# W_down of both sequences in one pass of seven block products, with its combinations made in the steps

## The chip, the core and the metric

The kernel runs on one core of a Trainium2 chip. The metric is the time of one execution on the device in microseconds; the median of several runs stands for a kernel. TensorE does the matrix products (in the profile PE, its weight loads PEld), VectorE is DVE, ScalarE is ACT, GpSimd is POOL, and SyncE (SP) issues nearly all transfers, one after the other from one queue.

## What is computed

One layer of a bidirectional encoder on two sequences with the same weights, `x_sample` (512 tokens) and `x_prompt` (1024 tokens), both preceded by 16 meta tokens. All is in 32-bit floats. What the change touches is the end of the layer and the last norm:

```python
D_MODEL = 1024; D_FF = 4 * D_MODEL
...
    x = x + mixed @ w_out
    a = jax.nn.relu(rmsnorm(x, g_mlp) @ w_up)
    return x + (a * a) @ w_down
...
    return rmsnorm(h, g_final)[:, N_META:]
```

## The kernel before

**The two sequences** run one after the other, the sample first. Each goes through projections, attention, the Fourier branch, the merge, `project_out` (W_out, the residual and the norm for the MLP) and the MLP. While the sample's MLP runs, `reading` takes in the prompt's tokens (load, norm, transposition), one tile at a time.

**Precision.** Every product of two 32-bit tiles is made from three matmuls: each operand is split into a high part (rounded by ScalarE, L151) and the low rest (a subtraction by GpSimd or DVE, L152), and `mm3` (L128) adds high x high, high x low and low x high into one PSUM bank. A matmul has a stationary operand of 128 x 128 and a moving one of 128 x 512. A weight block of 128 x 1024 numbers is 512 KB; `wtile` gives two buffers each for a raw block, its high and its low part (`w_raw`, `w_hi`, `w_lo`).

**The sample's MLP** (class `Mlp`) goes over the 4096 hidden channels in 32 blocks of 128. `up(f)` makes block f for all 512 tokens: 8 x 3 matmuls, relu on ScalarE (L1082), the square on DVE (L1083), and the split (L1084, L1085). After every two blocks `down` multiplies them by their two blocks of W_down: 4 tiles of tokens x 2 halves of the output, 6 matmuls each, and DVE adds each result to an accumulator in SBUF (L1131). The last `down` takes four blocks; beside it the four blocks of w_in for the prompt's V (`before_last`) are loaded and split, and the four tiles of tokens get their last norm and are stored.

**Combinations.** While W_down's blocks lie in SBUF for the sample, `combine` makes on GpSimd (L1100) the four block sums that the prompt's product needs, and stores them in DRAM (`wt`, 2 MB for each of eight groups u of 512 hidden channels).

**The prompt's MLP** (class `Halves`) makes products of 2 x 2 blocks with seven block products (Winograd's form): the tokens are cut into two halves of 512, the channels into two halves. `up` makes the hidden channels in 16 pairs, and stores for each group u the four quarters of the squared hidden and four sums of them in DRAM (`hidden_prompt`, L1461 and L1477). Its turn tiles (`take`, names x0 to x7, y0, y1, gain) hold the weights of W_up in turn.

**The prompt's W_down** (`start_down`, `fetch_down`, `down`) then goes through 7 x 8 steps: for each of the seven products n, over the eight groups u. A step loads one quarter or sum of the hidden (512 KB) and one block or combination of W_down (512 KB) (L1496), splits both, and does 4 tiles x 2 x 3 = 24 matmuls. The steps' split parts have four buffers, and `load(i + 3)` is called in step i. When the last u of a product is done, `evict` puts the four banks together into the accumulators. The last three steps of the last product are done tile by tile, and each tile is normed and stored (`finish`) at once.

**Order.** A planner orders the instructions of each engine ahead of time by their place in the program and by its own estimate of when each can start, so that an instruction can be put ahead of earlier ones that are not ready. `behind(marks)` and `pinned()` hold instructions behind what stands before them in the program on the same engine.

Of the kernel before, what the change touches and what calls it, by code (L numbers as in the profile page):

```python
# [17 lines left out]
F32 = mybir.dt.float32  # L18
# [50 lines left out]
class Layer:  # L69
    def __init__(self, tc, ctx, ins, outs):  # L70
# [17 lines left out]
        self.wt = []  # L88
# [239 lines left out]
    def run(self, order):  # L328
# [3 lines left out]
        for i, (name, T) in enumerate(order):  # L332
# [112 lines left out]
            mlp = self.Mlp(self, hp_, mp, name, T, h2T, acc)  # L445
# [18 lines left out]
            mlp.run(reading, before_last, gate, lambda: tile_("r1").bitcast(F32))  # L464
# [546 lines left out]
    def project_out(self, hp, p, x, T, m, wo, acc, mlp, marks):  # L1011
# [36 lines left out]
        mlp.load(2, self.pair(p, [128, 2, 512], "w", 2))  # L1048
# [5 lines left out]
    class Mlp:  # L1054
        G = 2
        NF = FF // 128

        def __init__(self, layer, hp, p, name, T, h2T, acc):
            self.layer, self.nc, self.hp, self.p, self.name, self.T, self.h2T, self.acc = layer, layer.nc, hp, p, name, T, h2T, acc
            self.w, self.hid = {}, {}  # L1060
            self.ups = [self.up(f) for f in range(self.NF)]

        def load(self, f, to=None):
            if f not in self.w:
                to = to and [x.rearrange("p a (k c) -> p (a k) c", c=128) for x in to]
                self.w[f] = self.layer.weights(self.layer.rows("w_up", f * 128), to)

        def up(self, f):
# [4 lines left out]
            hi, lo = (t.rearrange("p a b -> p (a b)") if len(t.shape) == 3 else t  # L1073
                      for t in self.layer.pair(self.hp, [128, T] if T == 512 else [128, 2, 512], "hid", 2 * self.G))
            self.hid[f] = hi, lo
            step = 256 if f < 3 and T == 512 else 512
            for c in range(T // step):
# [3 lines left out]
                r = self.p.tile([128, 512], F32, name="relu", bufs=2)[:, :step]  # L1081
                nc.scalar.activation(out=r, in_=ps, func=AF.Relu)  # L1082
                nc.vector.tensor_tensor(out=r, in0=r, in1=r, op=ALU.mult)  # L1083
                nc.scalar.copy(out=hi[:, cs], in_=r)  # L1084
                nc.vector.tensor_tensor(out=lo[:, cs], in0=r, in1=hi[:, cs].bitcast(F32), op=ALU.subtract)  # L1085
                yield

        def combine(self, g, even, odd):


            nc, wt = self.nc, self.layer.wt
            if g % 2 == 0:
                wt.append(self.layer.dram.tile([128, 2, 4, 512], F32, name=f"wt{g // 2}"))
            (b11, b12), (b21, b22) = ([x[:, i] for i in range(2)] for x in (even, odd))
            t = [self.hp.tile([128, D], F32, name="hn", bufs=2) for _ in range(2)]
            t1, t2, t3, t4 = (x[:, i * 512:(i + 1) * 512] for x in t for i in range(2))
            to = [wt[-1][:, g % 2, 2 * i:2 * i + 2].rearrange("p a b -> p (a b)") for i in range(2)]
            for i, ops in enumerate((((t1, b12, b11), (t2, b22, t1)), ((t3, b22, b12), (t4, b21, t2)))):
                for x in ops:
                    nc.gpsimd.tensor_tensor(out=x[0], in0=x[1], in1=x[2], op=ALU.subtract)  # L1100
                nc.sync.dma_start(to[i], t[i])
                yield

        def down(self, fs, last, gate):

            layer, nc, T, acc, hid = self.layer, self.nc, self.T, self.acc, self.hid
            w, raws = {}, []
            marks = layer.mark()
            for i, f in enumerate(fs):
                to = (layer.pair(self.p, [128, 2, 512], "w", 2 if T == 512 else 4) if i < 2 else  # L1110
                      tuple(gate()[:, :, :512] for _ in range(2)))
                raw = self.raws[i]().rearrange("p (a b) -> p a b", a=2)
                nc.sync.dma_start(raw, layer.ins["w_down"][f * 128:(f + 1) * 128, :].rearrange("p (a b) -> p a b", a=2))
                w[f] = [t.rearrange("p a b -> p (a b)") if T == 512 else t for t in layer.split_sb(raw, *to)]
                raws.append(raw)
            combining = chain(*(self.combine(fs[i] // 2, raws[i], raws[i + 1]) for i in range(0, len(fs), 2)))
            if last:
                for _ in combining:
                    pass
                with layer.behind(marks + layer.mark()):  # L1120
                    last()
                gain = layer.gain(self.p.tile([128, D], F32, name="gain", bufs=1), "g_final")
            for t in range(T // 128):
                ts = slice(t * 128, (t + 1) * 128)
                for half in range(2):
                    cs = slice(half * 512, (half + 1) * 512)
                    ps = layer.psum()
                    layer.mm3(ps, [(hid[f][0][:, ts], hid[f][1][:, ts], *(v[:, cs] if T == 512 else v[:, half] for v in w[f]))
                                   for f in fs])
                    with layer.tc.high_priority(offset=60) if last and t == T // 128 - 1 else nullcontext():  # L1130
                        nc.vector.tensor_tensor(out=acc[t][:, cs], in0=acc[t][:, cs], in1=ps, op=ALU.add)  # L1131
                with layer.pinned():
                    next(combining, None)
                if last:
                    o = self.hp.tile([128, D], F32, name="hn", bufs=2)
                    with layer.tc.high_priority(offset=60) if t == T // 128 - 1 else nullcontext():
                        layer.norm(acc[t], gain, o, junk=self.p.tile([128, D], BF16, name="junk", bufs=1))
                    nc.sync.dma_start(layer.outs[self.name][t * 128:(t + 1) * 128, :], o)

        def run(self, reading, before_last, gate, raw):  # L1140
            other = lambda: self.layer.wtile("raw", [128, D]).bitcast(F32)
            self.raws = [raw, lambda: self.p.tile([128, D], F32, name="gain", bufs=1), other, other]
            G, NF = self.G, self.NF
            for g in range(NF // G - 1):
                for f in range(g * G + (G if g else 0), (g + 2) * G):
                    for _ in self.ups[f]:
                        pass
                next(reading, None)
                if g < NF // G - 2:
                    self.down(range(g * G, (g + 1) * G), None, gate)  # L1150
            for _ in reading:
                pass
            self.down(range(NF - 2 * G, NF), before_last, gate)


class Halves:
# [18 lines left out]
    def run(self, right, hp, mp, m, wo):  # L1175
# [6 lines left out]
        raws = [list(layer.pair(mp, [128, 2, self.TH], "w", 2)) for _ in range(2)]  # L1182
        self.start_down(raws)
# [297 lines left out]
    DOWN = ((0, "b11", 0), (5, "t2", 1), (2, "b21", 0), (6, "t3", 1), (4, "t1", 0), (3, "t4", 1), (7, "b22", 0))  # L1481

    def block(self, b, u):

        if b[0] == "t":
            return self.layer.wt[u][:, :, int(b[1]) - 1]
# [4 lines left out]
    def fetch_down(self, i, raws):  # L1491

        n, u = self.steps[i]
        a, b, _ = self.DOWN[n]
        for raw, src in zip(raws, (self.hid[u][:, :, a], self.block(b, u))):
            self.nc.sync.dma_start(raw.bitcast(F32), src)  # L1496
        self.raws[i] = raws
# [8 lines left out]
    def down(self, p):  # L1506

        layer, nc, nt, TH, nu, steps = self.layer, self.nc, self.nt, self.TH, self.nu, self.steps
        nh = nt // 2
        three = lambda x: x.rearrange("p (a b) -> p a b", a=2)  # L1510
        got = {}

        def load(i):
            if i >= len(steps):
                return
            if i > 1:

                self.fetch_down(i, [layer.wtile(("raw", "hi", "lo")[(i - 2) % 3], [128, 2, 512]) for _ in range(2)])
            got[steps[i]] = [layer.split_sb(raw.bitcast(F32), *([three(x) for x in self.take(2)] if i < 2 else
                                                                layer.pair(p, [128, 2, 512], k, 4)), lo_engine=lo)  # L1520
                             for k, raw, lo in zip("hw", self.raws.pop(i), (nc.vector, None))]

        def product(ps, t, n, us):

            ts = slice(t * 128, (t + 1) * 128)
            layer.mm3(ps, [(h[0][:, k, ts], h[1][:, k, ts], w[0][:, k], w[1][:, k]) for h, w in (got[n, u] for u in us)
# [155 lines left out]
```

## Time and profile before

| | |
|---|---|
| median of 3 runs | 2016.33 us (2015.58 to 2018.94) |
| profiled execution: time, span | 2014.89 us, 2013.1 us |
| granted TensorE clock, mean | 0.993 |
| matmuls recorded | 9635 |
| TensorE busy | 1950.7 us, 97% of the span |
| DVE, ScalarE, GpSimd busy | 55%, 38%, 48% |
| moved by DMA | 326.50 MB, mean 162 GB/s |
| the sample's MLP | about 363 to 736 us of the span |
| the prompt's W_down | about 1697 to 2002 us |

The profile is one execution. The timeline gives the start of an instruction in us from the start of the span, its duration, engine and line, and what it writes and reads; `[x <-engine tile line]` is the idle time ahead of it and what ended it. A matmul's duration there (0.39 us) is its latency: matmuls overlap, and the distance between two starts is what one costs. SPq rows are issues of transfers.

### The profile page before, as it was taken

The page shows a single profiled execution, that of the slowest core. Times are in us where ns is not written, and L with a number is a line of the kernel's source. Part 1 is how long each engine was busy: PE and PEld are TensorE (multiplying, and loading weights), DVE is VectorE, ACT ScalarE, POOL GpSimd, SP SyncE. Part 2 cuts the span into 40 slices and gives each one's busy share as a digit, 9 for nine tenths or more (in the row PEclk, how much of TensorE's full clock was granted, in tenths as well). Part 3 has the DMA queues.
Part 4 walks back from the last instruction along what each step waited for, and adds up shares of the span by engine and source line. Part 5 has one row for each costly group of instructions (what it writes and reads, how often), then busy time and mean ns, then how long its engine had stood idle before and what let it go on. Part 6 is the DMA issues. An engine that isn't in the chain of part 4 may idle for free.

```text
span 2013.1 us, 26468 instructions
## 1 busy us (share of the span) xinstructions
PE 1950.7 (97%) x9635; PEld 1621.2 (81%) x9635; DVE 1105.3 (55%) x1916; ACT 757.2 (38%) x1325; POOL 958.9 (48%) x743
## 2 busy tenths in 40 slices
PE   6999999999999999999999998999999999999997
PEld 4887787888888878888888887887888888888886
DVE  6672445756665452666653326566656656443246
ACT  3564322433333322556552303124333333433342
POOL 3244535477766740223343226113978774644442
PEclk9999999999999999999999999999999999999999
DMA  6666772344554445555555544212454445876663
GB/s 204 168 167 216 217 217 91 124 155 151 165 166 135 157 148 197 129 130 136 141 184 161 133 114 144 110 63 84 173 172 167 167 159 188 304 245 197 193 193 122
DMA packets 275652, 326.50 MB, mean 162 GB/s; under 512 B 42872, under 2 KB 197240, under 8 KB 274968
## 3 DMA queue, kind: packets, MB, share of 16 engines
q1 hardware_dynamic: 261792, 303.92, 47.5%
q0 software_dynamic: 13728, 20.88, 4.5%
q8 instruction: 76, 1.25, 0.3%
q14 instruction: 56, 0.46, 0.1%
HBM read 235.67 MB, written 91.64 MB: 163 GB/s over the span
## 4 chain that ended last, share of the span: by engine, by line
PE 80%; DMA 6%; DVE 5%; issue 3%; POOL 3%; ACT 2%; SPq 1%; POOLq 0%; ACTq 0%; DVEq 0%
PE ps_mm L128 21%; PE ps_o L128 20%; PE ps_s L128 18%; PE ps_t L128 8%; PE ps_mm L487 2%; PE ps_mm L488 2%; PE ps_mm L489 2%; POOL w_lo L152 2%; PE ps_o L629 1%; DMA w_raw<-in_w_in 1%; DMA w_raw<-in_w_out 1%; PE ps_t L609 1%; DMA gain<-in_w_fnB 1%; PE ps_t L193 1%; DMA sin<-in_sin_prompt 1%
## 5 line engine op out<-in xcount | busy, mean ns | idle before, releaser
L152 POOL TENSOR_TENSOR w_lo<-w_raw,w_hi 128x1024 fp32r<-128x1024 f32 x84 | 213.1, 2545 | 211.4 <-ACT w_hi L151 186.6
L151 ACT CAST w_hi<-w_raw 128x1024 fp32r<-128x1024 f32 x100 | 104.7, 1048 | 155.4 <-PE ps_s L128 49.3
L487 PE MATMUL ps_mm<-hT,w_hi 128*128 128x512 f32 (+3 forms) x320 | 126.0, 394 | 0.0
L1083 DVE TENSOR_TENSOR relu<-relu 128x512 f32<-128x512 f32 (+1 forms) x35 | 64.7, 1849 | 108.5 <-ACT relu L1082 108.5
L488 PE MATMUL ps_mm<-hT,w_hi 128*128 128x512 f32 (+3 forms) x320 | 114.8, 359 | 0.0
L489 PE MATMUL ps_mm<-hT,w_lo 128*128 128x512 f32 (+3 forms) x320 | 114.7, 359 | 0.0
L603 ACT ACTIVATE sc<-sc,ast 128x288 f32<-128x288 f32 (+4 forms) x96 | 53.9, 561 | 76.9 <-DVE ast L601 76.7
L723 POOL MEMSET bm<- 64x96 f32 (+2 forms) x64 | 11.2, 175 | 144.5 <-DVE ast L601 99.8
L152 POOL TENSOR_TENSOR w_lo<-r,w_hi 128x1024 fp32r<-128x1024 f32 x15 | 36.8, 2453 | 88.0 <-ACT w_hi L151 88.0
L1330 POOL TENSOR_TENSOR x<-w_hi,x 128x512 fp32r<-128x512 f32 (+1 forms) x42 | 66.2, 1576 | 23.8 <-ACT x L1333 23.8
L629 PEld LDWEIGHTS ps_o<-pt,vb 104*64 104x64 f32 (+6 forms) x576 | 61.7, 163 | 11.4 <-POOL vb L566 4.6
L152 POOL TENSOR_TENSOR w_lo<-w_hi 128x1024 fp32r<-128x1024 f32 x18 | 45.4, 2521 | 49.1 <-ACT w_hi L151 45.8
L152 POOL TENSOR_TENSOR w_lo<-w_lo,w_hi 128x1024 fp32r<-128x1024 f32 x18 | 46.5, 2585 | 46.4 <-ACT w_hi L151 46.4
L489 PEld LDWEIGHTS ps_mm<-hT,w_lo 128*128 128x128 f32 x320 | 60.1, 188 | 8.6
L629 PE MATMUL ps_o<-pt,vb 104*64 104x128 f32 (+6 forms) x576 | 62.8, 244 | 3.7 <-POOL vb L566 2.0
L566 POOL TENSOR_TENSOR vb<-vr,vb 96x384 fp32r<-96x384 f32 (+4 forms) x48 | 48.6, 1032 | 35.6 <-ACT vb L565 29.0
L128 PE MATMUL ps_t<-gate,x 128*128 128x512 f32 x264 | 65.3, 396 | 0.0
L128 PE MATMUL ps_mm<-gate,x 128*128 128x512 f32 x256 | 64.3, 395 | 0.0
L488 PEld LDWEIGHTS ps_mm<-hT,w_hi 128*128 128x128 f32 x320 | 60.7, 190 | 1.7
L487 PEld LDWEIGHTS ps_mm<-hT,w_hi 128*128 128x128 f32 x320 | 60.6, 189 | 1.8
L601 DVE CUSTOM_DVE_ANT_0 sc<-ps_s,bm 128x288 f32<-128x288 f32 (+4 forms) x96 | 46.3, 482 | 24.7 <-PE ps_s L597 13.7
L128 PEld LDWEIGHTS ps_t<-gate,x 128*128 128x128 f32 x264 | 49.5, 188 | 12.2 <-DVE r_lo L1443 0.3
(664 smaller groups left out, 5866.1 us busy)
## 6 DMA issues: line engine op xcount, KB each, us to landing
w_raw<-in_w_in SPq DMA_DIRECT2D x56, 512.0 KB
w_raw<-in_w_up SPq DMA_DIRECT2D x34, 512.0 KB
wt<-hn SPq DMA_DIRECT2D x32, 512.0 KB
hidden_prompt<-h SPq DMA_DIRECT2D x32, 512.0 KB
w_hi<-hidden_prompt SPq DMA_DIRECT2D x20, 512.0 KB
w_raw<-hidden_prompt SPq DMA_DIRECT2D x18, 512.0 KB
w_lo<-hidden_prompt SPq DMA_DIRECT2D x18, 512.0 KB
w_raw<-in_w_out SPq DMA_DIRECT2D x16, 512.0 KB
```

Of the source, the lines that this page charges most:

```text
L128: self.nc.tensor.matmul(out, a, b, start=(i == 0 and not more), stop=(i == len(terms) - 1), skip_group_check=more)
L151: nc.scalar.copy(out=hi, in_=raw)
L152: (lo_engine or nc.gpsimd).tensor_tensor(out=lo, in0=raw, in1=hi.bitcast(F32), op=ALU.subtract)
L487: nc.tensor.matmul(ps, a[0], b[0], start=(kt == 0), stop=False)
L488: nc.tensor.matmul(ps, a[0], b[1], start=False, stop=False)
L489: nc.tensor.matmul(ps, a[1], b[0], start=False, stop=(kt == 7))
L566: nc.gpsimd.tensor_tensor(out=lo, in0=vs, in1=hi.bitcast(F32), op=ALU.subtract)
L601: nc.vector.tensor_tensor_reduce(out=sc[:, :W], in0=ps[:, :W], in1=bm[:, :W], scale=1.0, scalar=3e38, op0=ALU.add, op1=ALU.min, accum_out= ...
L603: nc.scalar.activation(out=sc[:, :W], in_=sc[:, :W], func=AF.Exp, bias=st[:, 0:1], scale=-1.0, accum_out=st[:, 1:2])
L629: nc.tensor.matmul(po[:m, j * 128:(j + 1) * 128], v, x, start=(i == 0), stop=(i == len(ops) - 1))
L1083: nc.vector.tensor_tensor(out=r, in0=r, in1=r, op=ALU.mult)
L1330: self.nc.gpsimd.tensor_tensor(out=to, in0=x, in1=y, op=op)
```

## The change

1. **The sample's hidden goes to DRAM.** Class `Mlp` becomes `Up`: `up(f)` ends with relu and square, and stores the block; after each pair four sums are made on DVE and stored too, so that `hidden_sample` has the same eight quarters and sums as the prompt's (halves of 256 tokens). `project_out` stores the sample's residual (`sum_sample`). The split of the hidden, the sample's `down`, its norms and its output stores leave this place. W_up's blocks with f % 4 > 1, and the last four, get their split parts in two further buffers. `before_last` comes ahead of the last four blocks.
2. **Combinations.** Only t2 is made beside the sample's W_up, and only for even u, on GpSimd. All others are made in the steps, by DVE adds on the loaded blocks (`parts`).
3. **One pass.** A step of `Halves.down` loads the sample's part (256 KB), the prompt's part (512 KB) and one to four blocks of W_down, and does six tiles of tokens, 36 matmuls. The split parts have three buffers instead of four, `load(i + 2)` is called in step i, and the loads from the third step on stand behind the last store of the hidden. Six banks are in use for a product, and the order of the seven products is another. The last norms and output stores of the sample come in this pass.

```diff
@@ run (both sequences)
-            mlp = self.Mlp(self, hp_, mp, name, T, h2T, acc)
+            self.short = mlp = self.Up(self, ap, hp_, mp, name, T, h2T)
...
-            mlp.run(reading, before_last, gate, lambda: tile_("r1").bitcast(F32))
+            mlp.run(reading, before_last)
@@ project_out (sample)
                 if half:
+                    nc.sync.dma_start(mlp.sums[t], acc[t])
@@ class Mlp -> Up
         def load(self, f):
             if f not in self.w:
+                to = None
+                if f % 4 > 1 or f >= self.NF - 4:
+                    to = [x.rearrange("p a (k c) -> p (a k) c", c=128) for x in self.layer.pair(self.p, [128, 2, 512], "w", 2)]
                 self.w[f] = self.layer.weights(self.layer.rows("w_up", f * 128), to)
...
+                nc.scalar.activation(out=r[:, cs], in_=ps, func=AF.Relu)
+                nc.vector.tensor_tensor(out=r[:, cs], in0=r[:, cs], in1=r[:, cs], op=ALU.mult)
                 yield
+            nc.sync.dma_start(to[:, 2 * odd:2 * odd + 2], two(r))
+            if odd:
...
+                for k, x, y, op in ((s1, a21, a22, ALU.add), (s2, s1, a11, ALU.subtract), (s3, a11, a21, ALU.subtract),
+                                    (s4, a12, s2, ALU.subtract)):
+                    nc.vector.tensor_tensor(out=k, in0=x, in1=y, op=op)
+                nc.sync.dma_start(to[:, 4:8], sums)
+        def combine(self):
...
+                if u % 2:
+                    continue
...
+                nc.sync.dma_start(even, w[g * 256:g * 256 + 128, :])
+                nc.sync.dma_start(odd[:, :512], w[g * 256 + 128:g * 256 + 256, 512:])
                 yield
+                nc.gpsimd.tensor_tensor(out=odd[:, :512], in0=odd[:, :512], in1=even[:, 512:], op=ALU.subtract)
+                nc.gpsimd.tensor_tensor(out=odd[:, 512:], in0=odd[:, :512], in1=even[:, :512], op=ALU.add)
+                nc.sync.dma_start(layer.t2[u][:, g % 2], odd[:, 512:])
+                yield
+        def run(self, reading, before_last):
+            combining = self.combine()
+            for g in range(self.NF // 2):
+                if g == self.NF // 2 - 2:
+                    for _ in reading:
+                        pass
+                    with layer.pinned():
+                        before_last()
+                for f in range(2 * g, 2 * g + 2):
+                    for _ in self.ups[f]:
+                        pass
                 with layer.pinned():
                     next(combining, None)
+                if g:
+                    next(reading, None)
@@ class Halves
-    DOWN = ((0, "b11", 0), (5, "t2", 1), (2, "b21", 0), (6, "t3", 1), (4, "t1", 0), (3, "t4", 1), (7, "b22", 0))
+    DOWN = ((0, "b11"), (2, "b21"), (5, "t2"), (6, "t3"), (3, "t4"), (4, "t1"), (7, "b22"))
+    ON_TOP = (1, 4, 6)
+    PARTS = dict(t1=(("b12", 1), ("b11", -1)), t2=(("b22", 1), ("b12", -1), ("b11", 1)), t3=(("b22", 1), ("b12", -1)),
+                 t4=(("b21", 1), ("b22", -1), ("b12", 1), ("b11", -1)))
+    def parts(self, b, u):
+        if u in layer.t2 and b in ("t2", "t4"):
+            return ([(self.w_down("b21", u), 1)] if b == "t4" else []) + [(layer.t2[u], -1 if b == "t4" else 1)]
+        return [(self.w_down(k, u), sign) for k, sign in self.PARTS.get(b, ((b, 1),))]
@@ down
+            return layer.wtile(("hi", "hi", "lo", "lo", "raw", "raw")[(self.streamed - 1) % 6], [128, 2, 512])
...
+                self.fetch_down(i, [lambda: p.tile([128, 2, SH], F32R, name="short", bufs=2),
+                                    lambda: p.tile([128, 2, TH], F32R, name="long", bufs=2)] + [stream] * 4)
...
+            for x, (_, sign) in zip(rest, self.parts(self.DOWN[n][1], u)[1:]):
+                nc.vector.tensor_tensor(out=rw, in0=rw, in1=x, op=ALU.add if sign > 0 else ALU.subtract)
...
+                ws, wl, ww = (layer.pair(p, [128, 2, w], k, 3) for k, w in (("hs", SH), ("h", TH), ("w", 512)))
...
-            with layer.behind(self.stored if i < 2 else []):
-                load(i + 3)
+            with layer.behind(self.stored if i < 6 else []):
+                load(i + 2)
...
             for t in range(nh):
-                product(banks[at][t], t, n, [u])
-            if u == nu - 1:
-                for t in range(nh):
+                product(banks[t], t, n, [u])
+                if u == nu - 1:
                     evict(n, t)
```

Here `nh` is 6, four tiles of the prompt's half and two of the sample's.

More of the change, by code (lines that the diff above doesn't have):

```diff
@@ L1047, in project_out @@
         mlp.load(1)
-        mlp.load(2, self.pair(p, [128, 2, 512], "w", 2))
+        mlp.load(2)
         for f in range(3):
@@ L1072, in up @@
             w = self.w.pop(f)
[L1073 to L1076, printed above, removed]
+            g, odd = divmod(f, 2)
+            if g not in self.r:
+                self.r[g] = [t.bitcast(F32) for t in self.layer.pair(self.hp, [128, T], "hid", 4)]
+            r = self.r[g][odd]
+            step = 256 if f < 3 else 512
             for c in range(T // step):
@@ L1086, in up @@
-                yield
[L1088 to L1101, printed above, removed]
-                yield
@@ L1104, in down @@
[L1104 to L1131, printed above, removed]
@@ L1133, in down @@
                     next(combining, None)
[L1134 to L1153, printed above, removed]
+                if g:
+                    next(reading, None)
@@ L1506, in down, with stream @@
     def down(self, p):
-        layer, nc, nt, TH, nu, steps = self.layer, self.nc, self.nt, self.TH, self.nu, self.steps
-        nh = nt // 2
-        three = lambda x: x.rearrange("p (a b) -> p a b", a=2)
+        layer, nc, TH, nu, steps = self.layer, self.nc, self.TH, self.nu, self.steps
+        short = layer.short
+        SH = short.T // 2
+        nl, ns = TH // 128, SH // 128
+        nh = nl + ns
+        tiles = [[(self.sums[h * nl + t], self.name, h * nl + t) for t in range(nl)] +
+                 [(short.sums[h * ns + t], short.name, h * ns + t) for t in range(ns)] for h in range(2)]
         got = {}
+        self.streamed = 0
+        def stream():
+            self.streamed += 1
+            return layer.wtile(("hi", "hi", "lo", "lo", "raw", "raw")[(self.streamed - 1) % 6], [128, 2, 512])
         def load(i):
@@ L1516, in load @@
             if i > 1:
[L1518 to L1521, printed above, removed]
-        def product(ps, t, n, us):
-            ts = slice(t * 128, (t + 1) * 128)
-            layer.mm3(ps, [(h[0][:, k, ts], h[1][:, k, ts], w[0][:, k], w[1][:, k]) for h, w in (got[n, u] for u in us)
-                           for k in range(2)], more=us[0] > 0 or n > 1 and self.DOWN[n][0] in (2, 3, 7))
@@ L1530, in down @@
+        def product(ps, t, n, us):
+            at = t if t < nl else t - nl
+            ts = slice(at * 128, (at + 1) * 128)
+            ops = []
+            for u in us:
+                s, l, w = got[n, u]
+                h = l if t < nl else s
+                ops += [(h[0][:, k, ts], h[1][:, k, ts], w[0][:, k], w[1][:, k]) for k in range(2)]
+            layer.mm3(ps, ops, more=us[0] > 0 or n in self.ON_TOP)
+        for i in range(2):
             load(i)
-        acc = [p.tile([128, D], F32, name=f"acc{t}") for t in range(nt)]
@@ L1544, in evict @@
         def evict(n, t):
-            ps = banks[self.DOWN[n][2]][t]
-            c1, c2 = acc[t], acc[nh + t]
+            ps = banks[t]
+            c1, c2 = (acc[h][t] for h in range(2))
             if n == 0:
```

106 lines of the change are left out of this document (63 added, 43 removed).

## The prediction

> **What bounds the kernel now.** I read the page first (engine totals and the forty slices), then the stretches of the two MLP stages, then the timeline of TensorE in each, the queue of transfers and the helpers. Busy time, instruction count:
>
> ```profile
> PE 1950.7 (97%) x9635; PEld 1621.2 (81%) x9635; DVE 1105.3 (55%) x1916; ACT 757.2 (38%) x1325; POOL 958.9 (48%) x743
> ...
> PE   6999999999999999999999998999999999999997
> ```
>
> Stretches: length, busy time of PE, PEld, DVE, ACT, POOL with counts, then granted clock, DMA share, GB/s.
>
> ```profile
> 362.00:700.00 338.00, 336.09 (x1582) 278.67 (x1581) 210.76 (x310) 120.45 (x176) 231.98 (x119) 1.00 0.47 154
> 700.00:736.00 36.00, 31.53 (x127) 24.41 (x126) 21.29 (x32) 10.93 (x14) 20.10 (x10) 0.91 0.48 154
> 1690.00:1990.00 300.00, 300.00 (x1323) 248.02 (x1322) 128.18 (x137) 118.48 (x124) 139.07 (x55) 1.00 0.67 217
> ```
>
> The sample's MLP (363 to 736 us) and the prompt's W_down (from 1697 us) are walls of matmuls: TensorE is busy all the time, the others half of it. In such a stage a removed matmul is worth its whole spacing. One place is not full: 700 to 736, where 4.5 us are idle and the clock is 0.91.
>
> **The price of a matmul, and how many go.** Timeline of TensorE: start, duration, what.
>
> ```profile
> 390.55 0.40 PE L128 MATMUL ps_o<-w_hi,hid_hi 128*128 128x512 f32 x1
> ...
> 401.46 3.90 PE L128 MATMUL ps_s<-gate,w_hi 128*128 128x512 f32 x16
> ...
> 706.58 0.40 PE L128 MATMUL ps_s<-w_hi,hid_hi 128*128 128x512 f32 x1
> ...
> 735.99 0.39 PE L128 MATMUL ps_mm<-w_hi,hT 128*128 128x512 f32 x1
> ...
> 1697.42 1.09 PE L128 MATMUL ps_mm<-x,x 128*128 128x512 f32 x4
> ...
> 1985.93 0.39 PE L128 MATMUL ps_mm<-w_hi,h_hi 128*128 128x512 f32 x1
> ```
>
> One W_down call of the sample on two blocks (4 tiles of tokens x 2 halves x 2 blocks x 3 products = 48 matmuls) takes 401.46 - 390.55 = 10.91 us, 0.2273 each. 53 steps of the prompt's pass (53 x 24 = 1272) take 288.51 us, 0.2268 each. Now the sample does 32 x 4 x 2 x 3 = 768 matmuls in W_down; by seven products of half size it does 7 x 16 x 2 x 3 = 672, in the prompt's steps and of the same shape. So 768 x 0.2273 - 672 x 0.2268 = 174.6 - 152.4 = **22.2 us less**, whatever the rest does. The prompt's 1344 matmuls stay.
>
> **The handover.** The sample's last W_down call (96 matmuls, 706.58 to 735.99) takes 29.4 us for 96 x 0.2273 = 21.8. What it waited for, and the helper that was late:
>
> ```profile
> PE ps_s L128 <- POOL gate L152: 2.3, 2, 2.0
> PE ps_s L128 <- POOL w_lo L152: 2.2, 2, 1.6
> ...
> 709.77 5.59 POOL L152 TENSOR_TENSOR gate<-w_raw,gate 128x1024 fp32r<-128x1024 f32 x2
> ```
>
> GpSimd was still making the low parts of W_down, behind the combinations. 4.5 us of it is the wait, the rest the lower clock after it. That call is gone: **7.6 us less**. What is late next: the four blocks of w_in for the prompt's V. They are now loaded from g = 14 on, through the two w_raw buffers, while W_up blocks 28 to 31 pass the same two. Before, in the queue, ACT and DVE:
>
> ```profile
> 712.60 15.14 SPq L145 DMA_DIRECT2D w_raw<-in_w_in  x5
> ...
> 716.31 1.04 ACT L151 CAST w_hi<-w_raw 128x1024 fp32r<-128x1024 f32 x1 [5.31 <-DMA w_raw<-in_w_in]
> ...
> 729.23 1.22 DVE L152 TENSOR_TENSOR r<-w_raw,r 128x1024 fp32r<-128x1024 f32 x1
> ```
>
> Four such blocks went from issue to split in 712.60 to 730.45, 17.9 us: 7.2 for the first (3.7 landing, 1.04, 2.4 on GpSimd) and some 3.5 for each next. Six (four of V, W_up 30 and 31) need 7.2 + 5 x 3.5 = 25 us. The cover is the matmuls of blocks 28 to 31, 4 x 5.55 (next fence) = 22.2, less some 4 us until the pinned queue lets the first one go. So about 6 us late, of which other token tiles' matmuls cover a part, then a spell of lower clock: between 0 and 9, I take **5 us back**. No cost at all needs W_up 30 and 31 to be in early; 17 us needs W_up 28 to queue behind all four of V (a rival below).
>
> **The sample's W_up alone.** Timeline of TensorE, then the queue, then one GpSimd combination:
>
> ```profile
> 516.02 5.58 PE ps_mm L128 x24
> 521.60 5.52 PE ps_s L128 x24
> ...
> 505.25 0.37 SPq L1113 DMA_DIRECT2D r<-in_w_down  x1
> ...
> 507.17 3.21 SPq L145 DMA_DIRECT2D w_raw<-in_w_up  x2
> ...
> 699.06 1.30 POOL L1100 TENSOR_TENSOR hn<-w_raw 128x512 f32<-128x512 f32 x1 [1.13 <-issue]
> ```
>
> A block is 24 matmuls, 5.55 us; a pair with the reading's transposes some 12 us instead of 22.9. Blocks are loaded as soon as a w_raw is free (507.17, 9 us ahead of 516.02); the change gives four places for split blocks instead of two, so one may be three blocks (16.6 us) late before TensorE sees it. Transfers for a pair: W_up 1 MB, hidden quarters 0.5, their sums 0.5, W_down's parts and t2 0.5, the reading 0.5 = 3.0 MB in 12 us, 260 GB/s, nine pairs long, against 154 now. The rows of what the transfers reach:
>
> ```profile
> 1710.00:1720.00 10.00, 10.00 (x45) 8.10 (x44) 7.06 (x4) 7.60 (x8) 7.81 (x3) 1.00 1.03 378
> ...
> 1730.00:1740.00 10.00, 10.00 (x46) 8.26 (x44) 2.45 (x2) 5.09 (x7) 5.70 (x3) 1.00 0.95 309
> ```
>
> So it fits, not by much. ACT's hi cast and DVE's lo subtract of the hidden are gone, four quarter-sized adds a pair and two combinations every second pair come. Bounds 0 to 11 (rival); I take **1 us**. The four stores of the sums lie in project_out, where W_up 0 and 1 are in long before: nothing, and if they were behind, one landing of 3.7 us.
>
> **The prompt's pass.** A step has 36 matmuls, 8.16 us instead of 5.44. Splitting: ACT casts 1.04 + 1.04 + 0.6; GpSimd 2.4; DVE 1.22 + 0.61, and 1.22 for each add that makes a combination, up to three in an odd t4 step: 5.5 of DVE and 2.4 of GpSimd. Bytes: 0.75 MB of hidden, 0.5 to 2 MB of W_down. The worst pair of steps (t4, even 1.75, odd 2.75 MB: 4.72 million bytes) asks 289 GB/s over 16.3 us, the others under 230. Six stream buffers hold just such a pair, so a transfer has about two steps to land. No wait of TensorE was seen from 1690 on with half this time for a step; **0 to 8, I take 0**. Evictions are spread behind six banks instead of four, and a bank is met again 5 x 1.36 us later; their DVE work has more room in a step than now. The beginning: only two steps are loaded ahead instead of three, and the third waits for the last store of the hidden:
>
> ```profile
> 1702.61 1.05 SPq L1477 DMA_DIRECT2D hidden_prompt<-h  x2
> ```
>
> 1703.7 + about 7 to land three tiles + 1.04 + 2.4 = 1714, wanted 1697.42 + 16.3 = 1713.7: **1 us**, up to 3. The end: pairs have 3 buffers instead of 4, and the last three steps run together, so the last step's split starts only when step 53 of 56 has ended: 3.1 us until its high, 5.5 until its low part, while the first tile has 16 matmuls, 3.6 us, without it, and other tiles more: **1 us** of 0 to 3.5. The tail after the last matmul is one tile's norm and store either way.
>
> **Sum.** -22.2 - 7.6 + 5 + 1 + 0 + 1 + 1 = -21.8. The profiled execution took 2014.9 (span 2013.1), the median of the runs is 2016.3, 1.4 above; so 2016.3 - 21.8 = **1994.5**. Its own range: from all covers held (-29.8, 1986.5) to the upper bounds of handover, start and end (9 + 1 + 3 + 3.5: 2003).
>
> **Rivals.**
> Handover in program order (0.12): if w_raw goes to V's four blocks ahead of W_up 28, TensorE stops after block 27 for about 4 + 7.2 + 4 x 3.5 = 25 us less what V's loads then no longer cost later: 17 instead of 5, 2006.5. For it: these loads stand ahead of W_up 28 in the program. Against: 507.17, where a load goes as soon as its buffer is free.
>
> One port for DVE and GpSimd (0.10). Rows of the last steps:
>
> ```profile
> 1962.54 2.40 POOL L152 TENSOR_TENSOR w_lo<-w_hi 128x1024 fp32r<-128x1024 f32 x1 [4.93 <-ACT w_hi L151]
> ...
> 1961.44 1.22 DVE L152 TENSOR_TENSOR h_lo<-w_hi,h_hi 128x1024 fp32r<-128x1024 f32 x1
> 1962.57 2.39 DVE L181 SCALAR_TENSOR_TENSOR st<-st 128x1 f32<-128x1 f32 x1
> ...
> 1965.00 0.15 DVE L182 SCALAR_TENSOR_TENSOR st<-st 128x1 f32<-128x1 f32 x1
> ```
>
> An operation on one column took 2.39 us instead of 0.15, as long as GpSimd's subtract beside it. So in a W_up pair with combinations their times add: GpSimd 2 x 2.4 + 2 x 1.3, DVE two squares 1.2, four sums 1.2, the reading's norm some 2.9 (one pass over 1024 columns and nine small ones) = 12.7 of 12 us; without them 10.1. If each norm also loses one subtract of 2.4, nine pairs average 13.8, 1.8 over, 16 us, of which the blocks in hand hide between nothing and all; with one of them (5.55) some 11 stay: 2005.5. The Trainium skill (SBUF — State Buffer, Who interferes with whom) states this as a rule: a VectorE instruction with two SBUF inputs and a GpSimd one that reads SBUF exclude each other, "an exclusive lock", the later one waiting out the earlier. By that rule the adds in the odd t4 steps, 7.9 of 8.16 us, would be the tight place as well. The row of 2.39 us agrees with it.
>
> The other side (0.07): W_up's loads stand behind the new stores in the one queue. A store of a pair's sums waits for its last matmul, relu, square and four adds; if the next pair's blocks are issued only behind it, TensorE waits 3.7 + 1.04 + 2.4 us less the blocks in hand. It decides from 1.6 us a pair (16 x 1.6 = 26 eats 21.8 and 4 more); with no block in hand it is 7.1 x 15 = 107, 2100. Against: the same planner puts W_up's loads ahead now.
>
> Transfers that never pass the 217 GB/s of the row from 1690 on (0.04): then t4 pairs take 21.7 us instead of 16.3, four times 5.4, and the nine pairs of W_up 14.5 instead of 12: 21.6 + 22.5 less the slack = about 24 more, no change (2016). Against: 309 and 378.
>
> **Numbers.** Forecast 0.67; program order 0.12; port 0.10; queue 0.07; transfers 0.04. Within 0.2% (4 us) is what a measurement here can't tell from no change. Faster 0.67 + 0.12 + 0.10 = 0.89; same 0.04; slower 0.07. The range runs from all covers held with 1.5 us of scatter (1985) to above the first two rivals (2011), which leaves out the last two and a little.
>
> **What would show it.** TensorE's matmuls fall by 96; steps of the last pass start 8.16 us apart; between the sample's last W_up and the prompt's first V product stands a wait of a few us for w_lo or w_hi; no waits in between W_up blocks; transfers at 250 GB/s or more there. Wrong, if TensorE waits for GpSimd or a transfer in most of the pairs or steps.

## The result, and the profile after

The changed kernel took 2039.3 us (median of 4 runs, 2036.2 to 2041.8), the kernel before 2016.6 us beside it (2015.6 to 2018.9): a ratio of 1.0111, 95% interval 1.0098 to 1.0123. So it is slower by 22.7 us where 21.8 less were forecast. The profiled execution took 2038.9 us (span 2037.1), at a mean granted clock of 0.981 instead of 0.993.

The page: busy time, share and instruction count, then two rows of the forty slices, TensorE and its clock.

```profile
PE 1934.6 (95%) x9539; PEld 1608.2 (79%) x9539; DVE 1133.0 (56%) x1939; ACT 740.3 (36%) x1316; POOL 814.6 (40%) x663
...
PE   6999999999499999999999999999999999979997
...
PEclk9999999999799999999999999999999999989999
```

96 matmuls fewer, as the change says (9635 - 9539), and TensorE is busy for 16 us less. But the wall has a hole in the eleventh slice and a dent in the thirty-sixth, with a lower clock in both. TensorE's waits, by what ended them (us in total, times, longest), from the sample's W_up to V, and then in the last pass:

```profile
PE ps_o L128 <- ACT w_hi L151: 26.4, 1, 26.4
...
PE ps_t L128 <- DVE u L1552: 12.0, 1, 12.0
PE ps_mm L128 <- POOL w_lo L152: 1.9, 1, 1.9
PE ps_o L128 <- DVE h L1552: 1.7, 1, 1.7
PE ps_s L128 <- POOL w_lo L152: 1.4, 1, 1.4
```

Two waits carry the loss. The first in the timeline of TensorE, of the transfer queue and of ScalarE:

```profile
530.75 1.98 PE L128 MATMUL ps_s<-gate,w_lo 128*128 128x512 f32 x8
559.12 5.51 PE L128 MATMUL ps_o<-gate,w_hi 128*128 128x512 f32 x16 [26.40 <-ACT w_hi L151]
...
582.60 0.39 PE L128 MATMUL ps_mm<-w_hi,hT 128*128 128x512 f32 x1
```

```profile
536.68 0.46 SPq L1121 DMA_DIRECT2D t<-acc  x1
537.23 10.62 SPq L145 DMA_DIRECT2D w_raw<-in_w_in  x4
553.65 1.45 SPq L145 DMA_DIRECT2D w_raw<-in_w_up  x2
```

```profile
542.91 1.04 ACT L151 CAST w_hi<-w_raw 128x1024 fp32r<-128x1024 f32 x1 [9.56 <-DMA w_raw<-in_w_in]
...
558.03 1.04 ACT L151 CAST w_hi<-w_raw 128x1024 fp32r<-128x1024 f32 x1 [4.91 <-DMA w_raw<-in_w_up]
```

TensorE had ended W_up block 27 at 532.7. The load of block 28 was not issued before 553.65: the queue first sent V's four blocks (537.23), and these stood behind the last stores of block 27. 26.4 us of wait, and 5.51 - 3.79 = 1.7 us more for the next 16 matmuls, at a lower clock (3.79 is what 16 take elsewhere), together some 28.3 with what follows.

The second, in the timeline of TensorE and of DVE, at the start of the fifth product (step 32 of 0 to 55):

```profile
1811.55 0.61 PE L128 MATMUL ps_mm<-w_hi,hs_lo 128*128 128x512 f32 x2
1824.20 0.76 PE L128 MATMUL ps_t<-w_hi,h_hi 128*128 128x512 f32 x1 [12.03 <-DVE u L1552]
```

```profile
1803.34 1.21 DVE L152 TENSOR_TENSOR h_lo<-long,h_hi 128x1024 fp32r<-128x1024 f32 x1
1807.76 1.23 DVE L1527 TENSOR_TENSOR w_raw<-w_raw,w_hi 128x1024 f32<-128x1024 f32 x1 [3.21 <-DMA w_hi<-in_w_down]
1809.66 1.23 DVE L1527 TENSOR_TENSOR w_lo<-w_lo 128x1024 f32<-128x1024 f32 x1 [0.68 <-DMA w_lo<-t]
1810.80 2.86 DVE L152 TENSOR_TENSOR hs_lo<-short,hs_hi 128x512 fp32r<-128x512 f32 x1
1813.59 1.21 DVE L152 TENSOR_TENSOR h_lo<-long,h_hi 128x1024 fp32r<-128x1024 f32 x1
1819.54 2.18 DVE L1527 TENSOR_TENSOR w_hi<-w_hi 128x1024 f32<-128x1024 f32 x1 [4.74 <-DMA w_hi<-in_w_down]
...
1823.38 1.27 DVE L1552 TENSOR_TENSOR u<-u,ps_t 128x512 f32<-128x512 f32 x2
```

The fifth product adds onto the banks of the fourth, so its first matmul needs the eviction of the first tile (1823.38). That tile's product had ended by 1806. In DVE's order the adds that make the combinations of later steps (L1527) stand ahead of it: the last one of step 33 (1807.76), the one of step 34 (1809.66) and two of step 35 (the first at 1819.54). They wait for blocks that are still on their way: 4.74 us idle at 1819.54, with the eviction ready behind. Busy time does not show this: DVE is at 56%.

### The profile page after: what moved, and what is told of

It reads as the page before. It is cut to its first block, busy times and chain, and to the rows that moved or that the text cites. A ratio compares the mean times of both kernels' runs of the same rounds, so it can differ in the third digit from the quotient of the medians.

```text
span 2037.1 us, 26463 instructions
## 1 busy us (share of the span) xinstructions
PE 1934.6 (95%) x9539; PEld 1608.2 (79%) x9539; DVE 1133.0 (56%) x1939; ACT 740.3 (36%) x1316; POOL 814.6 (40%) x663
## 4 chain that ended last, share of the span: by engine, by line
PE 69%; DVE 8%; DMA 7%; issue 7%; POOL 4%; ACT 3%; SPq 1%; POOLq 0%; ACTq 0%; DVEq 0%
PE ps_mm L128 19%; PE ps_o L128 17%; PE ps_s L128 14%; PE ps_t L128 9%; POOL w_lo L152 3%; PE ps_mm L487 2%; PE ps_mm L488 2%; PE ps_mm L489 2%; PE ps_o L629 1%; DMA w_raw<-in_w_out 1%; DMA w_raw<-in_w_in 1%; DVE st L181 1%; PE ps_t L609 1%; DVE st L182 1%; DMA gain<-in_w_fnB 1%
## 5 line engine op out<-in xcount | busy, mean ns | idle before, releaser
L152 POOL TENSOR_TENSOR w_lo<-w_raw,w_hi 128x1024 fp32r<-128x1024 f32 x84 | 219.6, 2617 | 311.4 <-ACT w_hi L151 270.6
L151 ACT CAST h_hi<-long 128x1024 fp32r<-128x1024 f32 x54 | 56.9, 1053 | 193.9 <-issue 54.6
L152 DVE TENSOR_TENSOR h_lo<-long,h_hi 128x1024 fp32r<-128x1024 f32 x54 | 69.6, 1288 | 83.2 <-ACT h_hi L151 83.2
L128 PE MATMUL ps_o<-gate,w_hi 128*128 128x512 f32 (+1 forms) x192 | 45.2, 385 | 26.4 <-ACT w_hi L151 26.4
L152 DVE TENSOR_TENSOR hs_lo<-short,hs_hi 128x512 fp32r<-128x512 f32 x54 | 52.6, 974 | 27.8 <-ACT hs_hi L151 26.7
L151 ACT CAST hs_hi<-short 128x512 fp32r<-128x512 f32 x54 | 33.6, 622 | 93.1 <-PE ps_t L128 24.5
L488 PEld LDWEIGHTS ps_mm<-hT,w_hi 128*128 128x128 f32 x320 | 61.0, 191 | 1.8
L128 PE MATMUL ps_t<-w_hi,h_hi 128*128 128x512 f32 x128 | 50.9, 398 | 12.0 <-DVE u L1552 12.0
```

The costliest lines, as they stand in the source:

```text
L128: self.nc.tensor.matmul(out, a, b, start=(i == 0 and not more), stop=(i == len(terms) - 1), skip_group_check=more)
L151: nc.scalar.copy(out=hi, in_=raw)
L152: (lo_engine or nc.gpsimd).tensor_tensor(out=lo, in0=raw, in1=hi.bitcast(F32), op=ALU.subtract)
L488: nc.tensor.matmul(ps, a[0], b[1], start=False, stop=False)
```

## The experiments

Two theories. *Order of buffers*: the 26.4 us come from the two `w_raw` buffers being given out in program order, to V's blocks first. *Order on DVE*: the 12.0 us come from adds ahead of the eviction. The rivals are the pinned queue itself for the first, and a supply of blocks that is too slow in any order for the second. All times below stand beside runs of the kernel before on the same chip, whose medians there were 2016.4 to 2017.2 us.

**V's raw blocks in other buffers**

```diff
-    self.wv[q] = self.value_weights(q, ...)
+    self.wv[q] = self.value_weights(q, ..., raw=ap.tile([128, D], F32, name=f"acc{2 + q % 2}"))
```

> Raw blocks of V's four loads go to the free accumulator buffers acc2 and acc3 instead of w_raw; they stay pinned behind the last stores of hidden block 27. Theory 'rotation' (TensorE stood for 26.4 us ahead of W_up 28 because the two w_raw buffers are given out in program order, to V's four blocks first): W_up 28 and 29 are issued ahead of V's blocks, the wait of ps_o for w_hi falls from 26.4 to 0 to 3 us, V's first product starts 20 to 28 us earlier; 2011 to 2019 us against 2039. Of the 28.3 us of the handover up to 8 may come back as a wait for V's own low parts. Rival 'pin' (the pinned queue itself holds everything behind the stores): the wait stays above 15 us, 2030 or more.

Measured: 2013.6 us (10 runs), 0.9991 of before (0.9978 to 1.0004); 25.7 less than the changed kernel. The queue:

```profile
528.92 0.38 SPq L145 DMA_DIRECT2D w_raw<-in_w_up  x1
529.47 0.46 SPq L1096 DMA_DIRECT2D hidden_sample<-hid_hi  x1
536.14 0.37 SPq L145 DMA_DIRECT2D w_raw<-in_w_up  x1
...
538.49 2.30 SPq L145 DMA_DIRECT2D acc<-in_w_in  x2
```

Every W_up block is issued ahead of V's, though these are pinned where they were. TensorE's waits in this stretch are then 0.2 us in the last W_up block, and 1.7 and 0.8 us at V's first tile. The theory of the buffers holds, the rival of the pin falls.

**V's loads not pinned, same buffers**

```diff
-                    with layer.pinned():
-                        before_last()
+                    before_last()
```

> V's four loads are no longer pinned; they keep the w_raw buffers and their place in the program ahead of W_up 28. Theory 'rotation': the order of the buffers stays, but V's loads can start among blocks 24 to 27, so the whole chain of eight loads through two buffers (about 3.5 us each, 28 us) starts some 20 us earlier; the wait falls from 26.4 to 0 to 8 us, and blocks 24 to 27 may lose 0 to 4 us; 2011 to 2022 us. Theory that the transfers or GpSimd's splits are simply too slow for eight blocks beside the stores of the hidden: stalls of more than 12 us in sum remain, spread over blocks 25 to 31; above 2025.

Measured: 2016.3 us (10 runs, 2013.1 to 2029.4), 1.001 (0.9991 to 1.0029). TensorE's waits:

```profile
PE ps_o L128 <- ACT w_hi L151: 10.2, 1, 10.2
PE ps_o L128 <- DVE u L1551: 5.1, 1, 5.1
...
PE ps_t L128 <- DVE u L1551: 2.9, 1, 2.9
```

V's loads now start among blocks 24 to 27, but W_up 28 still has its turn after all four: 10.2 us are left, a little over the 0 to 8 of the expectation. The evictions show how much of an accident their place is: after a change in another stage the waits for the third and the fourth product's evictions, 0.4 and 12.0 us in the changed kernel, are 5.1 and 2.9.

**The adds held behind the evictions**

```diff
+            with layer.behind(self.evicted):
                 for x, (_, sign) in zip(rest, ...):
                     nc.vector.tensor_tensor(out=rw, in0=rw, in1=x, ...)
...
                 if u == nu - 1:
                     evict(n, t)
+                    self.evicted = layer.mark((mybir.EngineType.DVE,))
```

In the fourth product the two adds of an eviction change places, so that the mark lies on the one that reads the bank.

> DVE's adds that make combinations of later steps are held behind the evictions of the step that ends a product; nothing else moves. Theory 'order on DVE' (TensorE stood 12.0 us at the fourth to fifth product, plus 2.5 at a lower clock, because the eviction that frees its bank stood behind adds of two steps ahead whose blocks had not landed): the wait for the eviction goes; the low part of that step's prompt tile, which is itself late by about 3 us behind the adds of the next step, remains as 2 to 4 us; 2027 to 2031 us. Rival 'supply' (blocks come too late for the t4 steps in any order): a wait of 8 us or more moves to w_hi, w_lo or h_lo in the same steps; 2036 or more.

Measured: 2022.7 us (6 runs), 1.0027 (1.0016 to 1.0039); 16.7 less than the changed kernel, more than expected. DVE at the same place:

```profile
1805.20 0.69 DVE L1553 TENSOR_TENSOR u<-u,ps_t 128x512 f32<-128x512 f32 x1 [0.46 <-PE ps_t L128]
...
1809.96 1.23 DVE L152 TENSOR_TENSOR h_lo<-long,h_hi 128x1024 fp32r<-128x1024 f32 x1
...
1812.60 1.22 DVE L1528 TENSOR_TENSOR w_lo<-w_lo 128x1024 f32<-128x1024 f32 x1
1813.74 0.69 DVE L152 TENSOR_TENSOR hs_lo<-short,hs_hi 128x512 fp32r<-128x512 f32 x1
1814.34 1.22 DVE L1528 TENSOR_TENSOR w_hi<-w_hi 128x1024 f32<-128x1024 f32 x1
```

Each eviction now waits only for its own bank, and no wait of TensorE is left there. I had expected the low part of that step's own tile (h_lo) to stay late by 2 to 4 us. That was a misreading: counted from the start of the pass, the h_lo at 1813.59 in the changed kernel is that of step 33, and step 32's had been made at 1803.34, some 7 us before the step could start. (In this run step 32's comes at 1795.09, and 1809.96 is step 34's.) So there was nothing to stay late, and the gain is larger: 12.0 and 2.5 us at this place and 0.9 at the third product's evictions, where no wait is left either, make 15.4 of the 16.7. No wait moved to w_hi or w_lo, so with the evictions first the supply was not short.

**Only as many stream buffers as a step has blocks**

```diff
-        self.raws[i] = raws = [x() if callable(x) else x for x in raws][:len(sources)]
+        self.raws[i] = raws = [x() if callable(x) else x for x in raws[:len(sources)]]
```

> A step takes only as many of the six stream buffers as it has blocks (one to four) instead of always four. Theory 'supply': loads of the t4 steps are issued up to two steps earlier, their adds on DVE no longer wait 3 to 5 us each, and the 12.0 us wait at the start of the fifth product shrinks to 0 to 5 although the order on DVE is of the same kind; 2025 to 2033 us. Theory 'order on DVE' alone: the adds that stand ahead of the eviction still wait for blocks that their buffers can't take earlier (the raw buffer is the place where the sum is made, and goes only with the split); the wait stays within 8 to 14 us; 2035 to 2041.

Measured: 2032.9 us (4 runs), 1.0085 (1.0069 to 1.0102); 6.4 less than the changed kernel. TensorE:

```profile
1814.27 0.47 PE L128 MATMUL ps_t<-w_hi,h_hi 128*128 128x512 f32 x1 [1.39 <-DVE u L1552]
```

The wait of 12.0 us shrank to 1.4, but one of 2.9 us for an eviction came up in the first step of the sixth product, and the one for the third product's evictions grew from 0.4 to 0.8. Both theories have a part: the adds ahead of the eviction cost as much as their blocks are late, and the blocks were late because every step took four of the six stream buffers, also a step with one block. Sooner buffers ease it, the order removes it.

**Both orders mended**

> Both changes together: V's raw blocks in acc2 and acc3, and the adds behind the evictions. If the two stalls are independent, their gains add: 2039.3 - 25.7 - 16.7 = 1997, range 1994 to 2000, which is 19 below the kernel before. If the second only shows because the first delays or spreads the transfers, less than 30 of 42 comes: above 2009. What is left of the forecast's terms at this point: V's own low parts some 3.6 (forecast 5), the third step 3.8 (forecast 1), the last split 1.5 (forecast 1), the evictions of the sixth product 1.9 (forecast 0).

Measured: 1998.8 us (4 runs), 0.9913 (0.9899 to 0.9928). The gains of the two nearly add up (25.7 + 16.7 = 42.4; 40.5 came), as they should if the stalls are independent.

**The same, with the stream buffers as needed**

> As the one with both changes, with only as many stream buffers taken as a step has blocks. If supply limits nothing once the evictions stand first, no change: within 2 us of the one with both, about 1997. If the remaining small waits of the t4 steps came from late blocks, 2 to 4 us less; if the planner orders other DVE work ahead of evictions again (as in the run with this edit alone, 2.9 us ahead of the sixth product), 2 to 4 us more.

Measured: 2001.0 us (4 runs), 0.9921 (0.9906 to 0.9935). In the pass its waits are the same ones as without the edit (1.0 and 1.9 at the third step, 1.7 and 1.4 near the end), so once the evictions stand first, earlier buffers bring nothing there. The 2 us more are not settled by the runs; in the profiled execution they are at V's first tile, where a lower clock follows the waits, as it does not in the run without the edit.

**V's buffers, and the adds on GpSimd**

```diff
-                nc.vector.tensor_tensor(out=rw, in0=rw, in1=x, ...)
+                nc.gpsimd.tensor_tensor(out=rw, in0=rw, in1=x, ...)
```

> V's raw blocks in acc2 and acc3, and the adds of the combinations on GpSimd instead of DVE (not held behind anything). Theory 'order on DVE': DVE's queue has nothing left that waits for blocks of later steps except the low parts, so the 12.0 us wait falls to below 4 us. But GpSimd has then, in an odd t4 step, a subtract of 2.4 and three adds of about 2.6 us (1.30 for half the columns): 10.2 us for a step of 8.16, four such steps between even ones of 5.0: the pair has 15.2 of 16.3 us, so 0 to 4 us of waits for w_lo in these steps. 1998 to 2004 in all. If GpSimd becomes the bound (adds slowed by the port that it shares with DVE): waits for w_lo of 3 us or more in each odd step, above 2008.

Measured: 2048.0 us (4 runs), 1.0149 (1.0132 to 1.0166): 34 more than the 2013.6 with V's buffers alone and the adds on DVE. Theory 'order on DVE' had 1998 to 2004; the time lies where the other side put it, above 2008. TensorE's waits in the pass, and GpSimd:

```profile
PE ps_t L128 <- POOL w_lo L152: 27.7, 12, 3.9
PE ps_s L128 <- POOL w_lo L152: 6.4, 5, 1.7
```

```profile
1820.46 2.96 POOL L1528 TENSOR_TENSOR w_hi<-w_hi 128x1024 f32<-128x1024 f32 x1 [3.88 <-DMA w_hi<-in_w_down]
1823.50 2.37 POOL L1528 TENSOR_TENSOR w_hi<-w_hi,w_lo 128x1024 f32<-128x1024 f32 x1
1825.83 2.34 POOL L152 TENSOR_TENSOR w_lo<-w_raw,w_hi 128x1024 fp32r<-128x1024 f32 x1
```

The wait for the eviction is gone, as the order theory says. But now the split of a step stands behind adds of later steps, which wait for their blocks (3.88 us at 1820.46), and it does so in step after step. An add took 2.4 to 3.0 us where 2.6 was expected, and GpSimd still idles for blocks between its instructions (from 1800 to 1840 it is busy for 28.3 of 40 us). So it isn't busy time alone that decides here either: the same inversion has moved to the engine that every step depends on.

**Third step loaded ahead of the pass, norms of the sixth product behind its evictions**

```diff
-        for i in range(2):
+        for i in range(3):
             load(i)
...
-                load(i + 2)
+                if i:
+                    load(i + 2)
...
-                finish(1, t)          # in evict, sixth product
...
+            if (n, u) == (5, nu - 1):
+                with layer.behind(layer.mark((mybir.EngineType.DVE,))):
+                    for t in range(nh):
+                        finish(1, t)
```

(on top of both orders mended)

> As the one with both changes, and two small ones more: the third step is loaded ahead of the pass (its block of W_down then goes ahead of the last stores of the hidden, its hidden parts still behind them), and the norms of the sixth product's tiles are held behind all its evictions. Theory 'named waits': the 2.9 us for w_hi and w_lo of the third step falls to 0 to 1 with most of its spell at a lower clock, and the 1.7 us ahead of ps_o goes; 4 to 6 us less than the one with both, 1991 to 1993. Rival: the hidden's parts of the third step, issued where they were, are as late as the block (they land within 1 us of it): 1.9 us only, and 1995.

Measured: 1994.0 us (4 runs), 0.989 (0.9875 to 0.9905); 4.8 less. Of the third step's waits 0.4 is left, the one in the first step of the seventh product is gone. That is near the forecast's 1994.5, but with five edits that the changed kernel doesn't have, so the agreement is luck and confirms no term of the sum.

**V's blocks one pair of W_up blocks earlier; the last two steps by tiles instead of three**

```diff
-                if g == self.NF // 2 - 2:
+                if g == self.NF // 2 - 3:
```

```diff
-        apart = 3
+        apart = 2
```

Each alone on top of the last:

> As the fastest so far (both changes, third step early, norms late), with V's four blocks loaded one pair of W_up blocks earlier (ahead of block 26 instead of 28). Theory: the 1.8 and 0.8 us that V's first tile still waits for its third block's high and low parts, and the 0.4 us ahead of them, are there because these two blocks pass acc2 and acc3 a second time; 11 us more of cover takes all of it: 3 to 4 us less, 1990 to 1991. Rival: 2 MB more of transfers in a pair that already moves some 260 GB/s pushes W_up blocks late: waits of 1 us or more for w_hi or w_lo in blocks 26 to 29, and the sum is within 1 us of 1994.

> As the fastest so far, with the last two steps done tile by tile instead of the last three. Theory of the end by the forecast (the last step's low part is 1.4 us late because its pair of buffers comes free only when step 53 of 56 has ended, and nothing else matters): the wait goes, 1992.5. Rival: the norm of a tile takes DVE about 3.7 us (0.68 for the eviction, nine small ones of 0.19, 1.28 for the scaling, and gaps), and the tiles come every 2.7 us instead of 4.1, so six norms queue: the end of the last matmul is 1.4 us earlier but the tail after it grows from 11 to 14 or 16; 1995 to 1998.

Measured: 1994.3 us (4 runs, 1989.5 to 1995.3) and 1994.4 us (4 runs): neither differs from 1994.0 in the medians. In the traces each did what it was to do: V's first tile waits for nothing in the first (whose profiled execution was its fastest); in the second the wait of the last split is gone and the tail after the last matmul is 10.7 us (10.9 without), so the rival of norms that queue falls. Since the medians didn't settle it, the two together:

> V's blocks one pair earlier and the last two steps tile by tile, together, on the version with the other four edits. In the traces of the two alone the wait of V's first tile (about 4 us) and that of the last split (1.4 us) were gone, while the medians (1994.3 and 1994.4) did not differ from the version without them (1994.0). If the traces tell it right and the medians were scatter: 1988 to 1991. If the time that is freed comes back elsewhere (the runs' scatter hides a cost of V's transfers beside W_up's): 1993 to 1995.

Measured: 1987.8 us (4 runs, 1986.4 to 1990.1), 0.9856 (0.984 to 0.9873), 29.0 less than the kernel before. That is just under the 1988 to 1991 that the traces had promised, and clear of the other side's 1993 to 1995; why neither edit showed alone no run settles. TensorE on the page of its profile, and the one wait that is left in the last blocks of the sample's W_up and at V:

```profile
PE 1929.0 (97%) x9539; PEld 1605.5 (81%) x9539; DVE 1141.5 (57%) x1939; ACT 740.4 (37%) x1316; POOL 809.3 (41%) x663
...
PE   6999999999999999999999999999999999999997
```

```profile
550.20 3.96 PE L128 MATMUL ps_o<-gate,w_hi 128*128 128x512 f32 x16 [1.34 <-ACT w_hi L151]
```

In the pass, from the third step to the last matmul, TensorE waits for nothing.

## Why the prediction was wrong

Where the time went, by stretches of the span: up to V's first product -153.4 (735.99 before, 582.60 after; forecast -176.2); from there to the pass +1.3 (forecast 0); the pass to the end +176.0 (forecast +154.4). Their sum is the 24.0 us between the spans.

- **The price of the matmuls, -22.2, and the sample's last W_down call, -7.6: right.** With the stalls taken out the kernel is 29.0 faster, and these two are 29.8. No run separates one from the other.
- **The handover, 5 back (0 to 9): failed, 28.3.** The failing sentence is the one against the rival of program order, "where a load goes as soon as its buffer is free". The row at 507.17 shows a load that had its turn. It doesn't show whose turn it is when two kinds of blocks pass the same two buffers, and there V's four came first. So this rival (0.12) was the mechanism, and its gross price of 25 us was near the 26.4 measured. What failed in it was the next step, "less what V's loads then no longer cost later", which made it 17: nothing was paid back, and the clock took 2 more. With own buffers for V the handover cost some 4 us, near the 5, but that is luck: it is V's third block that is late there (1.7 and 0.8 us), not W_up's blocks in a chain of six.
- **The pass, "0 to 8, I take 0": failed, about 17.** 12.0 + 2.5 at a lower clock, 0.9 at the third product's evictions, 1.9 in the first step of the seventh product. I weighed DVE's 5.5 us of work against 8.16 us of a step and said that the evictions "have more room in a step than now". The room was there; the order was not. Adds that wait for transfers were put ahead of an eviction that was ready, and DVE sat idle for 4.74 us at 1819.54 without taking it. "No wait of TensorE was seen from 1690 on" was no evidence: in the kernel before, DVE had no adds of freshly loaded blocks in these steps.
- **"Six stream buffers hold just such a pair": wrong.** The code takes four of them in every step and drops those it doesn't need, so they turn over in one and a half steps. This is what made the adds' blocks late; mending it alone was worth 6.4 us.
- **The start, 1 (up to 3): 4.1.** 0.2 and 1.9 us of wait for the third step's block, and 2 at a lower clock; I had the wait and left out the clock.
- **The end, 1 (0 to 3.5): right**, 1.4 for the last split. W_up alone, 1: it cost 0; its window shows TensorE full at 262 GB/s:

```profile
390.00:510.00 120.00, 119.39 (x559) 98.12 (x559) 105.08 (x160) 49.58 (x76) 68.08 (x31) 1.00 0.83 262
```

So the rivals of the queue and of slow transfers did not come. The port did: in this stretch a square of 128 x 512 on DVE took 2.90 us at 424.50, beside a subtract of GpSimd (423.45 to 426.84), and 0.68 at 437.94 with GpSimd idle. No wait of TensorE in W_up followed from it, and its price there was 0 instead of 11. In the pass a split of the same size took 2.86 us instead of 0.69 (1810.80 above, beside GpSimd's subtract, and 1813.74 in the run with the adds held); it stands among the rows ahead of the late eviction, and what it added to the 12.0 us no run separates.

With the measured terms the sum is -22.2 - 7.6 + 28.3 + 0 + 17 + 4.1 + 1.4 + 1.3 = +22.3, against 24.0 in the spans; the 1.7 left are not explained. Of the signs that I named, the 96 matmuls, the 8.16 us of a step and the 250 GB/s came, and the sign of being wrong, waits for GpSimd or a transfer in most of the pairs or steps, did not: two single stalls were enough. The chance of 0.07 for slower was too low because two faults of order add up: either of them alone left the kernel at 0.9991 or 1.0027 of before, and only both make it slower by more than 1%. One I had as a rival and underpriced, the other I had not at all, and the rivals were weighed as if no two could come together.

## What to carry to other kernels

When a change puts instructions that wait for transfers on an engine that also frees the banks or makes the splits, ask what stands in front of whom in that engine's order; busy shares say nothing about it, and it is cheap to hold the waiting kind behind the urgent one. When two streams of loads share a rotating set of buffers, as V's and W_up's blocks do here, the turn goes by the order in the program, so the stream that is needed later has to come later in it or have buffers of its own. Price a stall of ten microseconds or more with some 2 more for the clock after it: here 1.7 behind 26.4, 2.5 behind 12.0 and 2.1 behind 10.2.

## What the runs showed of the hardware

The clock after a wait: the last three columns are the granted clock, DMA share and GB/s, for the stretch behind the wait of 12.0 us, and for the one behind the third step's waits.

```profile
1824.20:1829.20 5.00, 5.00 (x13) 3.95 (x14) 4.56 (x7) 0.00 (x0) 0.00 (x0) 0.54 0.94 328
...
1564.90:1569.40 4.50, 4.50 (x14) 3.58 (x13) 3.70 (x3) 3.69 (x5) 2.39 (x1) 0.62 0.97 327
```

The Trainium skill (TensorE: Matmul & The Clock Gate, What's actually happening) says that an idle window of about 3.4 us halves the clock. The 0.54 behind 12.0 us agrees. In the second row some 2.1 us of waiting (0.2 and 1.9) were enough for a spell of 0.62, less than the page says is needed. At the same place, waits of 1.1 and 1.9 us in the run with V's raw buffers alone were followed by such a spell too (0.62 from 1540.54 to 1545.04), and waits of 1.0 and 1.9 with both orders mended by none (1.00 from 1541.64 to 1546.14). What decides between the two no run here shows.
